# A 31-tap depthwise convolution: 8 of 31 taps on TensorE as diagonal matmuls, against 17 of 31 in four token phases

## The chip, the cores and the metric

The kernel runs on one core of one Trainium2 chip. The metric is the device time of the whole program in microseconds (us), as the median of several runs; a profile of one further execution gives the trace. The core's engines each run their own instruction stream in order: TensorE (PE, with its weight loads shown as PEld), VectorE (DVE), ScalarE (ACT), GpSimd (POOL) and SyncE (SP), from whose queue the DMA transfers of this kernel are issued. An engine waits for another by semaphores.

## The reference

Two layers of a network run over 1024 latent tokens and 128 context tokens with 1024 features. Only the mixer of the second (odd) layer matters here. It projects 1024 features to 1536: 512 conv inputs `a`, 512 gates, 512 pool inputs.

```python
def depthwise_conv(x, w, b):
    K = w.shape[0]                      # 31 taps
    y = lax.conv_general_dilated(x, w[:, None, :], window_strides=(1,),
                                 padding=[(K // 2, K // 2)],
                                 dimension_numbers=("NWC", "WIO", "NWC"),
                                 feature_group_count=x.shape[-1])
    return y + b

def odd_mixer(h, w_in, w_dw, b_dw, g_cn, w_pool, s_pool, w_out):
    z = h @ w_in
    a, gte, p = jnp.split(z, [CONV_W, 2 * CONV_W], axis=-1)   # 512, 512, 512
    conv = a * jax.nn.sigmoid(gte)
    conv = depthwise_conv(conv, w_dw, b_dw)
    conv = jax.nn.silu(rms_norm(conv, g_cn))
    pool = multi_scale_pool(p).reshape(B, L, POOL_GROUPS, POOL_CH)
    pool = jnp.einsum("blgc,gcd->blgd", pool, w_pool).reshape(B, L, POOL_W) * s_pool
    return jnp.concatenate([conv, pool], axis=-1) @ w_out
```

The rest of the program is the first layer's mixer (attention and a gated unit), a feed-forward part with a 3-tap convolution in each layer, and norms. Both kernels run it from the same code.

## The kernel before, in words

All activations lie with features on the 128 partitions and tokens along the free axis, in three blocks of 384, 384 and 386 tokens (`BLK`). Matmuls work on pairs of rounded fp32 tiles: each operand is split into a high part (ScalarE copies it to the format `F32R`) and a low part (VectorE subtracts), and `mm3` (L76 to L78) multiplies high by high, high by low and low by high into one PSUM tile. `split` (L83, L84) does this for activations, `unit` and `unit_split` (L58, L66, L67) for weights: a load by SP into a staging tile `raw` of the pool `wraw`, and a split into `wt`. Diagonals built by GpSimd used a tile of the same staging pool.

`odd` is the mixer. It runs twelve projections in the order conv 0, conv 1, pool 0, pool 1, conv 2, pool 2, pool 3, conv 3; a conv has two (gates and values), a pool group one. `proj` makes one: for each token block, 24 matmuls into an `ips` tile of PSUM and an evacuation: `sg` (sigmoid, L1079), `cv` (value times gate, L1093, VectorE), or `xp` (L1116). `cv` holds 128 channels with padding, 1198 wide. The output of a conv, `co`, is 1168 wide.

A conv of 128 channels is shared between two engines. The last 8 taps are matmuls: `conv_prep` lets GpSimd build 8 diagonal 128x128 matrices `dg` (L1157), splits them to `dp` and splits `cv` to `cs`; `conv_pe` multiplies 8 diagonals with 8 shifted views of `cs`, for three stretches of columns (390, 390, 388), into `cps` tiles which ScalarE evacuates into `co` with the bias (L1174). The other 23 taps are `conv_steps`: each is one VectorE instruction `co = cv * w + co` over 1168 columns (L1181). They come after `conv_pe` in the program, for they add to its result.

The order of the work is that of the program, as a scheduler with priorities lays it on each engine. Two lists spread work over it: `fill` holds the taps, and `drip(n)` emits n of them behind each projection block; `pend` holds the call that starts a conv's matmuls (`conv_go`), which is taken from the list in block `GOB` (1) of the next projection.

Then come two halves of the output projection: `out_half` with the pool groups' half first (`pool_out` splits the pooled sums to `ph`, multiplies with a 128x128 matrix into `pp`, and evacuates to `h`, L1224 and L1225), then the conv half, whose input `conv_tail` makes from `co` with a norm over the channels. In the first `out_half` the call `mid` issues conv 3's matmuls between the pool products and the output tiles `ops`.

## Time and profile before

| | |
|---|---|
| time, median of 3 runs | 2802.07 us (2801.71 to 2804.49) |
| profiled execution, its own time | 2798.91 us |
| span of its instructions | 2797.1 us |
| mean granted TensorE clock | 0.985 |
| the odd mixer in it | from 1589 us (first `ips` matmul) to some 1970 us |
| conv matmuls `cps` | 288, from 1635.1 to 1818.3 us |
| conv taps on VectorE | 92, 133.2 us busy |

Times in the trace are counted from the span's start. A row of a stretch gives each engine's busy time in it with the count of instructions in brackets, then the clock that TensorE was granted (1.00 is full), the busy share of the DMA engines and the bytes moved. A row of a tile gives the instructions that touch it: line, engine, operation, count, then minimum, median and maximum duration in ns, and the first and last start. A row of the timeline is start, duration, engine, line, operation, and in square brackets the idle time before it and what ended that. Matmuls overlap in the pipe, so their pace is the distance of successive starts, not the duration.

### The profile page before, as it was taken

Reading aid. Unit: us, or ns where it says so; the run is one execution under the profiler, and the core shown is the slowest. Engines: PE = TensorE matmul, PEld = TensorE weight load, DVE = VectorE, ACT = ScalarE, POOL = GpSimd, SP = SyncE. Lnnn points to the kernel's source line nnn. Section 1 sums busy time; section 2 is a strip of 40 time slices with the busy share of each in tenths; the row PEclk is TensorE's granted clock in tenths of the full one; section 3 lists DMA queues with packets and bytes.
Section 4 is the critical chain, followed back from the end, with each engine's and each line's share of the span. In section 5 each row is a group of like instructions: output and inputs, shape, how many; then the busy total and the mean of one; then the engine's idle time right before and its main releaser. Section 6 shows DMA issues by size and latency. Waiting matters only on the chain.

```text
span 2797.1 us, 38522 instructions
## 1 busy us (share of the span) xinstructions
PE 2702.6 (97%) x15444; PEld 2622.6 (94%) x15444; DVE 1889.4 (68%) x3120; ACT 1010.8 (36%) x1798; POOL 375.6 (13%) x433
## 2 busy tenths in 40 slices
PE   7999989999999999999999999989999999999999
PEld 3897978889999999999999999888999999999999
DVE  5873799998787788855453878887555455554445
ACT  3543278882343222222223331225422222222331
POOL 2354155540200010000000200002000000000000
PEclk9999999999999999999999999999999999999999
DMA  7254210007143444311111011011011111111111
GB/s 277 71 154 112 86 32 23 25 1 234 53 128 114 131 133 128 119 48 46 38 46 38 10 46 39 27 39 38 31 38 46 38 46 39 45 37 40 46 46 68
DMA packets 92851, 192.64 MB, mean 69 GB/s; under 512 B 9472, under 2 KB 43136, under 8 KB 92672
## 3 DMA queue, kind: packets, MB, share of 16 engines
q1 hardware_dynamic: 92672, 190.18, 21.3%
q8 instruction: 122, 2.00, 0.3%
q14 instruction: 57, 0.47, 0.1%
HBM read 170.20 MB, written 19.95 MB: 68 GB/s over the span
## 4 chain that ended last, share of the span: by engine, by line
PE 83%; DVE 10%; DMA 3%; ACT 2%; issue 1%; POOL 1%; SPq 0%; DVEq 0%; POOLq 0%; ACTq 0%
PE fps L76 13%; PE fps L77 13%; PE fps L78 13%; PE ops L76 8%; PE ops L78 8%; PE ops L77 8%; PE av L982 2%; DMA mraw<-in_wmod_dram 2%; PE ptp L971 1%; DVE macc L157 1%; PE ips L76 1%; PE ips L77 1%; PE ips L78 1%; PE Sa L995 1%; PE mps L126 1%
## 5 line engine op out<-in xcount | busy, mean ns | idle before, releaser
L76 PE MATMUL fps<-h,wt 128*128 128x384 f32 (+1 forms) x2112 | 711.8, 339 | 1.6 <-ACT z L401 1.2
L77 PE MATMUL fps<-h,wt 128*128 128x384 f32 (+1 forms) x2112 | 713.0, 338 | 0.0
L78 PE MATMUL fps<-h,wt 128*128 128x384 f32 (+1 forms) x2112 | 712.7, 338 | 0.0
L379 DVE SCALAR_TENSOR_TENSOR x<-ops,mod,x 128x384 f32<-128x384 f32 (+1 forms) x832 | 395.6, 513 | 235.3 <-PE ops L78 233.8
L67 DVE TENSOR_TENSOR wt<-raw,wt 128x1024 fp32r<-128x1024 f32 (+2 forms) x177 | 216.8, 1235 | 385.1 <-ACT wt L66 384.6
L77 PEld LDWEIGHTS fps<-h,wt 128*128 128x128 f32 x2112 | 398.6, 189 | 0.3
L76 PEld LDWEIGHTS fps<-h,wt 128*128 128x128 f32 x2112 | 396.2, 188 | 2.5 <-ACT z L401 1.5
L78 PEld LDWEIGHTS fps<-h,wt 128*128 128x128 f32 x2112 | 398.1, 189 | 0.0
L78 PE MATMUL ops<-act,wt 128*128 128x384 f32 (+1 forms) x1056 | 358.2, 339 | 0.0
L77 PE MATMUL ops<-act,wt 128*128 128x384 f32 (+1 forms) x1056 | 357.0, 338 | 0.0
L76 PE MATMUL ops<-act,wt 128*128 128x384 f32 (+1 forms) x1056 | 355.4, 339 | 0.0
L401 ACT ACTIVATE z<-fps 128x384 f32<-128x384 f32 (+1 forms) x264 | 129.0, 493 | 602.9 <-PE fps L78 602.6
L66 ACT ACTIVATE wt<-raw 128x1024 fp32r<-128x1024 f32 (+2 forms) x177 | 182.8, 1047 | 440.1 <-PE ops L78 316.2
L157 DVE SCALAR_TENSOR_TENSOR macc<-mraw,sc,macc 128x512 f32<-128x512 f32 x280 | 214.5, 796 | 42.1 <-DMA mraw<-in_wmod_dram 41.7
L76 PEld LDWEIGHTS ops<-act,wt 128*128 128x128 f32 x1056 | 199.6, 189 | 0.0
L77 PEld LDWEIGHTS ops<-act,wt 128*128 128x128 f32 x1056 | 198.7, 188 | 0.0
L78 PEld LDWEIGHTS ops<-act,wt 128*128 128x128 f32 x1056 | 198.6, 188 | 0.1
L1181 DVE SCALAR_TENSOR_TENSOR co<-cv,c_odw,co 128x1168 f32<-128x1168 f32 x92 | 133.2, 1451 | 19.1 <-ACT co L1174 18.2
L76 PE MATMUL ops<-h,wt 128*128 128x384 f32 (+1 forms) x384 | 132.7, 351 | 7.0 <-ACT h L83 5.4
L83 ACT ACTIVATE act<-c 128x1154 fp32r<-128x1154 f32 x44 | 51.5, 1171 | 227.9 <-DVE c L422 183.5
L77 PE MATMUL ops<-h,wt 128*128 128x384 f32 (+1 forms) x384 | 132.2, 344 | 0.9 <-DVE h L84 0.9
L410 DVE SCALAR_TENSOR_TENSOR c<-z,fdw,c 128x1153 f32<-128x1153 f32 x88 | 125.7, 1429 | 8.6 <-ACT c L408 7.7
(275 smaller groups left out, 4578.0 us busy)
## 6 DMA issues: line engine op xcount, KB each, us to landing
raw<-in_fin_dram SPq DMA_DIRECT2D x88, 512.0 KB, 3.6
mraw<-in_wmod_dram SPq DMA_DIRECT2D x160, 256.0 KB, 2.8
raw<-in_fout_dram SPq DMA_DIRECT2D x44, 512.0 KB, 3.5
mraw<-in_wmod_dram SPq DMA_DIRECT2D x16, 512.0 KB, 8.8
fold<-macc SPq DMA_DIRECT2D x14, 512.0 KB, 2.9
macc<-fold SPq DMA_DIRECT2D x56, 128.0 KB, 3.3
x<-in_xt_dram SPq DMA_DIRECT2D x4, 1536.0 KB, 10.3
raw<-in_odin_dram SPq DMA_DIRECT2D x12, 512.0 KB, 3.5
```

Source lines behind the costliest of these rows:

```text
L66: nc.scalar.activation(wt[:, 0, :n], raw[:, :n], AF.Copy)
L67: nc.vector.tensor_tensor(out=wt[:, 1, :n], in0=raw[:, :n], in1=wt[:, 0, :n].bitcast(F32), op=ALU.subtract)
L76: mm(out, wh, ah, start=start, stop=False)
L77: mm(out, wh, al, start=False, stop=False)
L78: mm(out, wl, ah, start=False, stop=stop)
L83: ins = nc.scalar.activation(hi, src, AF.Copy)
L157: nc.vector.scalar_tensor_tensor(out=a[:, c, :], in0=raw, scalar=self.sc[:, k, c:c + 1], in1=a[:, c, :], op0=ALU.mult, op1=ALU.add)
L379: nc.vector.scalar_tensor_tensor(out=xs, in0=ps[:, o:o + w], scalar=self.mod[l][:, gch * 8 + m, c:c + 1], in1=xs, op0=ALU.mult, op1=ALU.add)
L401: nc.scalar.activation(z[:, c0:c0 + n], ps[:, :n], AF.Copy)
L410: nc.vector.scalar_tensor_tensor(out=c[:, 1:T], in0=z[:, 0:T - 1], scalar=w[:, l, ti, 0:1], in1=c[:, 1:T], op0=ALU.mult, op1=ALU.add)
L982: nc.tensor.matmul(av[:, :256].rearrange("p (j t) -> p j t", j=2), V[:, kt, h, :], rhs, start=(kt == 0 and part == 0), stop=(kt == 8 and p ...
L1181: nc.vector.scalar_tensor_tensor(out=o, in0=cv[:, j:j + COW], scalar=dw[:, j:j + 1], in1=o, op0=ALU.mult, op1=ALU.add)
```

## The change

17 of the 31 taps (14 to 30) go to TensorE. The operands are laid out anew: four token phases (token number modulo 4) of 32 channels each stand on the 128 partitions, for four groups of 32 channels in turn. One 128x128 matrix then mixes four input phases into four output phases and covers up to four taps; five of them (`NM`), on views shifted by one, cover 17 taps. The matrices of a group (128x640 fp32, 328 KB, `odiag`) are made on the host as constants and loaded, 16 times in all.

For each conv, `conv_prep` now lets GpSimd copy `cv` into four phases (`by4`), writes that to DRAM (`cvx`), reads it back in four transfers with phases on the partitions (`xr`), and splits that to `xs`. `conv_pe` gives four steps. Step g loads the matrices of group g into a staging tile, splits them to `dp`, makes 15 matmuls of 128x292 into one `cps` tile and copies it to `yo`. After the fourth, `yo` goes to DRAM (`cvy`), comes back in four transfers as `yb`, and `conv_merge` adds it to `co` on VectorE with a stride of four. The tiles `by4`, `xr`, `yo`, `yb` and the pool's `win` have one tag and one buffer (`by4`), and `dp` has one.

The 14 taps left no longer wait for the matmuls: the first writes `co` with the bias (a `tensor_scalar`), and the merge adds the matmuls' part. `pend` gives one step per projection block, after `SKIP` = 2 empty ones; conv 3's steps stand in the first output half, one behind each output tile after `SKIP3` = 4 empty ones. `pool_windows` works in place, every second `ph` uses the tag `dp`, and the tiles `hb` are as wide as their block.

```diff
-                            if b == GOB and pend:
-                                pend.pop()()
+                            if pend:
+                                pend.pop(0)()
...
-                        while len(self.fill) > 31 - NPE:
+                        while len(self.fill) > 8:
...
                     def conv(i):
                         cv = conv_in(i)
-                        ops = self.conv_prep(cv, dw[:, i, :], pdt)
-                        pend.append(lambda: conv_go(i, cv, ops))
+                        self.fill += self.conv_steps(co[:, i, :], cv, dw[:, i, :])
+                        xs = self.conv_prep(i, cv, pdt)
+                        pend.extend([lambda: None] * SKIP + conv_go(i, xs))
...
+    def conv_prep(self, i, cv, pool):
+        by4 = pool.tile([P, 4, XN], F32, tag="by4", bufs=1, name=self.nm("by4"))
+        nc.gpsimd.tensor_copy(by4, cv[:, J0:J0 + 4 * XN].rearrange("p (n s) -> p s n", s=4))
+        d = self.dram.tile([P, 4, XN], F32, name=f"cvx{i}")
+        nc.sync.dma_start(out=d, in_=by4)
+        xr = pool.tile([P, 4, XN], F32, tag="by4", bufs=1, name=self.nm("xr"))
+        for q in range(4):
+            nc.sync.dma_start(out=xr[32 * q:32 * q + 32, :, :], in_=d[:, q, :].rearrange("(g c) n -> c g n", c=32))
+        xs = pool.tile([P, 2, 4, XN], F32R, tag="cs", bufs=1, name=self.nm("xs"))
+        self.split(xs[:, 0], xs[:, 1], xr)
+        return xs
+
+    def conv_pe(self, i, xs, pool, done):
...
+        def step(g):
+            if not yo:
+                yo.append(pool.tile([P, 4, YN], F32, tag="by4", bufs=1, name=self.nm("yo")))
+            raw = self.wraw.tile([P, 1024], F32, tag="raw", name=self.nm("raw"))
+            nc.sync.dma_start(out=raw[:, :NM * P], in_=self.ap["odiag"][4 * i + g])
+            wt = pool.tile([P, 2, NM * P], F32R, tag="dp", bufs=1, name=self.nm("dp"))
+            self.unit_split(wt, raw, NM * P, None)
+            ps = self.gp.tile([P, 512], F32, tag="gp", name=self.nm("cps"))
+            for m in range(NM):
+                self.mm3(ps[:, :YN], wt[:, 0, m * P:(m + 1) * P], wt[:, 1, m * P:(m + 1) * P],
+                         xs[:, 0, g, m:m + YN], xs[:, 1, g, m:m + YN], m == 0, m == NM - 1)
+            nc.scalar.activation(yo[0][:, g, :], ps[:, :YN], AF.Copy)
+            if g == 3:
+                d = self.dram.tile([P, 4, YN], F32, name=f"cvy{i}")
+                nc.sync.dma_start(out=d, in_=yo[0])
+                yb = pool.tile([P, 4, YN], F32, tag="by4", bufs=1, name=self.nm("yb"))
+                for h in range(4):
+                    nc.sync.dma_start(out=yb[32 * h:32 * h + 32, :, :], in_=d[:, h, :].rearrange("(q c) n -> c q n", c=32))
+                done(yb)
...
+    def conv_merge(self, o, yb):
+        o4 = o.rearrange("p (n q) -> p q n", q=4)
+        self.nc.vector.tensor_tensor(out=o4, in0=o4, in1=yb, op=ALU.add)
...
-            ph = tp.tile([P, 2, BW], F32R, tag="ph", name=self.nm("ph"))
+            ph = tp[g % 2].tile([P, 2, BW], F32R, tag=("ph", "dp")[g % 2], bufs=1, name=self.nm("ph"))
...
-NPE = 8
+NM = 5
+NPE = 4 * NM - 3
+J0 = 31 - NPE
+YN = COW // 4
+XN = YN + NM - 1
```

Three places show how the instructions stand on the engines. The numbers behind a tile's name tell tiles apart; they differ between the kernels.

The first is TensorE where a conv's matmuls begin or go from phase to phase. Before, at conv 1's start in the middle of the first pool projection (`ips_15650`, `ips_15756`: its token blocks 1 and 2), the three `cps` tiles of 24 matmuls each share one `dp`:

```order
L78 MATMUL ips_15650<-h_1132_6920,wt_15520 128x384
L76 MATMUL cps_15676<-cs_15613,dp_15610 128x390
L76 MATMUL cps_15702<-cs_15613,dp_15610 128x390
L76 MATMUL cps_15728<-cs_15613,dp_15610 128x388
L76 MATMUL ips_15756<-h_1133_6921,wt_15520 128x386
L77 MATMUL ips_15756<-h_1133_6921,wt_15520 128x386
```

After, from phase 0 to phase 1 of conv 0 (`cps_15446` with `dp_15443`, then `cps_15505` with `dp_15502`, and the next projection `ips_15524`):

```order
L77 MATMUL cps_15446<-xs_15349,dp_15443 128x292
L78 MATMUL cps_15446<-xs_15349,dp_15443 128x292
L76 MATMUL cps_15505<-xs_15349,dp_15502 128x292
L77 MATMUL cps_15505<-xs_15349,dp_15502 128x292
L76 MATMUL ips_15524<-h_1132_6920,wt_15355 128x384
```

The first two matmuls of a phase moved up to directly behind the last of the phase before, which used the same buffer of `dp`; 24 projection matmuls follow, and then the phase's other 13.

On ScalarE at the same place, before (the split of `dp_15610` for conv 1 stands behind the evacuations of conv 0's three tiles):

```order
L1079 ACTIVATE sg_15348<-ips_15380 128x384
L66 ACTIVATE wt_15619<-raw_15617 128x1024
L1174 ACTIVATE co<-cps_15406,c_odw 128x390
L1174 ACTIVATE co<-cps_15432,c_odw 128x390
L1174 ACTIVATE co<-cps_15458,c_odw 128x388
L83 ACTIVATE dp_15610<-dg_15608 128x1024
```

and after, the whole of conv 0 and the beginning of conv 1 (`yo_15440` is conv 0's output, `dp_15736` the first matrices of conv 1):

```order
L83 ACTIVATE xs_15349<-xr_15344 128x1184
L1185 ACTIVATE yo_15440<-cps_15446 128x292
L66 ACTIVATE dp_15502<-raw_15500 128x640
L1185 ACTIVATE yo_15440<-cps_15505 128x292
L66 ACTIVATE dp_15552<-raw_15550 128x640
L66 ACTIVATE wt_15647<-raw_15645 128x1024
L1185 ACTIVATE yo_15440<-cps_15555 128x292
L66 ACTIVATE dp_15603<-raw_15601 128x640
L66 ACTIVATE wt_15772<-raw_15770 128x1024
L1116 ACTIVATE xp_15644<-ips_15650 128x384
L1185 ACTIVATE yo_15440<-cps_15606 128x292
L66 ACTIVATE dp_15736<-raw_15734 128x640
```

Each split of the next phase's matrices now stands behind the evacuation of the phase before it.

The second place is the turn from conv 0 to conv 1. Before, SP's queue holds only loads of weights (`raw<-in_odin_dram`) there. After:

```order
L1188 DMA cvy_15623<-yo_15440 128x1168
L1178 DMA raw_15801<-in_odiag_dram 128x640
L1178 DMA raw_15851<-in_odiag_dram 128x640
L1191 DMA yb_15625<-cvy_15623 32x4x292 x4
L1160 DMA cvx_15634<-by_2183_15632 128x1184
L1163 DMA xr_15636<-cvx_15634 32x4x296 x4
```

and on TensorE, after, conv 1's first matmul (`cps_15739`, which reads `xs_15641`, the split of `xr_15636`):

```order
L77 MATMUL ips_15706<-h_1133_6921,wt_15471 128x386
L78 MATMUL ips_15706<-h_1133_6921,wt_15471 128x386
L76 MATMUL cps_15739<-xs_15641,dp_15736 128x292
L76 MATMUL ips_15775<-h_1131_6919,wt_15647 128x384
L77 MATMUL ips_15775<-h_1131_6919,wt_15647 128x384
```

Conv 0's way out through DRAM and conv 1's way in stand one after the other in the queue, with two loads of matrices between. On TensorE 46 projection matmuls (22 of `ips_15678`, 24 of `ips_15706`) lie between conv 0's last matmul and conv 1's first.

The third is VectorE behind the last projection, where conv 2's or conv 3's taps (L1181 before, L1202 and L1204 after) share it with the pool's `ph` and `h`. Before:

```order
L1093 TENSOR_TENSOR cv_16480<-ips_16558,sg_16390 128x128
L1181 SCALAR_TENSOR_TENSOR co<-cv_15993,c_odw,co 128x1168
L84 TENSOR_TENSOR ph_16611<-pd,ph_16611 128x384
L84 TENSOR_TENSOR ph_16620<-pd,ph_16620 128x384
L1181 SCALAR_TENSOR_TENSOR co<-cv_15993,c_odw,co 128x1168
L84 TENSOR_TENSOR cs_16591<-cv_16480,cs_16591 128x1198
L1225 SCALAR_TENSOR_TENSOR h_1131_6919<-pp_16614,c_odw,h_1131_6919 128x384
```

After:

```order
L1093 TENSOR_TENSOR cv_16539<-ips_16615,sg_16452 128x128
L67 TENSOR_TENSOR wt_16560<-raw_16558,wt_16560 128x512
L1202 TENSOR_SCALAR co<-cv_16539,c_odw 128x1168
L84 TENSOR_TENSOR ph_16671<-pd,ph_16671 128x384
L1204 SCALAR_TENSOR_TENSOR co<-cv_16539,c_odw,co 128x1168
L1249 SCALAR_TENSOR_TENSOR h_1131_6919<-pp_16683,c_odw,h_1131_6919 128x384
L84 TENSOR_TENSOR ph_16698<-pd,ph_16698 128x384
L1249 SCALAR_TENSOR_TENSOR h_1131_6919<-pp_16674,c_odw,h_1131_6919 128x384
L1204 SCALAR_TENSOR_TENSOR co<-cv_16539,c_odw,co 128x1168
```

Conv 3's own taps moved up to this place, one for every one or two steps of the pool's chain, 11 of them ahead of the first output tile; conv 2's are done by then.

More of the change, by code (lines that the diff above doesn't have):

```diff
@@ L554, in out_half @@
         make(0)
-        if mid:
-            mid()
         if not late:
@@ L577, in out_half @@
                         self.out_tile(x, l, 2, b, m, terms)
+                        if mid:
+                            mid.pop(0)()
                         self.drip(drip)
@@ L1130, in odd @@
                     cv = conv_in(3, last)
-                    ops = self.conv_prep(cv, dw[:, 3, :], pdt)
+                    self.fill += self.conv_steps(co[:, 3, :], cv, dw[:, 3, :])
+                    xs3 = self.conv_prep(3, cv, pdt)
                 wps = units.pop()
@@ L1136, in odd @@
                     self.out_half(x, l, ap["odout"][1], hb, 4,
-                                  lambda b: self.at(PRP, self.pool_out, b, pd, dw, hb[b][:, :, 4:8, :], tp, wps), drip=DRIP2, ws=units,
-                                  mid=lambda: conv_go(3, cv, ops), outer=True)
+                                  lambda b: self.at(PRP, self.pool_out, b, pd, dw, hb[b][:, :, 4:8, :], (tp, pdt), wps), drip=DRIP2, ws=units,
+                                  mid=[lambda: None] * SKIP3 + conv_go(3, xs3), outer=True)
                 pdp.close()
@@ L1150, in odd @@
                                       late=True, extra=extra)
-    def conv_prep(self, cv, dw, pool):
+    def conv_prep(self, i, cv, pool):
         nc = self.nc
-        dg = self.wraw.tile([P, NPE, P], F32, tag="raw", name=self.nm("dg"))
-        nc.gpsimd.tensor_tensor(out=dg, in0=self.ident.unsqueeze(1).to_broadcast([P, NPE, P]),
-                                in1=dw[:, 31 - NPE:31].unsqueeze(2).to_broadcast([P, NPE, P]), op=ALU.mult)
-        dp = pool.tile([P, 2, NPE, P], F32R, tag="dp", bufs=1, name=self.nm("dp"))
-        self.split(dp[:, 0], dp[:, 1], dg)
-        cs = pool.tile([P, 2, CVW], F32R, tag="cs", bufs=1, name=self.nm("cs"))
-        self.split(cs[:, 0, :], cs[:, 1, :], cv)
-        return dp, cs
@@ L1165, in conv_pe @@
-    def conv_pe(self, o, ops, dw):
-        dp, cs = ops
-        for c1, c2 in ((0, 390), (390, 780), (780, COW)):
-            ps = self.gp.tile([P, 512], F32, tag="gp", name=self.nm("cps"))
-            for a in range(NPE):
-                j = 31 - NPE + a
-                self.mm3(ps[:, :c2 - c1], dp[:, 0, a, :], dp[:, 1, a, :], cs[:, 0, c1 + j:c2 + j], cs[:, 1, c1 + j:c2 + j],
-                         a == 0, a == NPE - 1)
-            self.nc.scalar.activation(o[:, c1:c2], ps[:, :c2 - c1], AF.Identity, bias=dw[:, 31:32])
+        by4 = pool.tile([P, 4, XN], F32, tag="by4", bufs=1, name=self.nm("by4"))
@@ new lines, in conv_prep @@
+        self.split(xs[:, 0], xs[:, 1], xr)
+        return xs
+    def conv_pe(self, i, xs, pool, done):
+        nc = self.nc
+        yo = []
+        def step(g):
[5 more added lines that the diff above has]
+            self.unit_split(wt, raw, NM * P, None)
+            ps = self.gp.tile([P, 512], F32, tag="gp", name=self.nm("cps"))
+            for m in range(NM):
[9 more added lines that the diff above has]
+                done(yb)
+        return [lambda g=g: step(g) for g in range(4)]
@@ L1180, in tap @@
         def tap(j):
-            nc.vector.scalar_tensor_tensor(out=o, in0=cv[:, j:j + COW], scalar=dw[:, j:j + 1], in1=o, op0=ALU.mult, op1=ALU.add)
+            if j == 0:
+                nc.vector.tensor_scalar(out=o, in0=cv[:, 0:COW], scalar1=dw[:, 0:1], scalar2=dw[:, 31:32], op0=ALU.mult, op1=ALU.add)
+            else:
+                nc.vector.scalar_tensor_tensor(out=o, in0=cv[:, j:j + COW], scalar=dw[:, j:j + 1], in1=o, op0=ALU.mult, op1=ALU.add)
         return [lambda j=j: tap(j) for j in range(31 - NPE)]
+    def conv_merge(self, o, yb):
+        o4 = o.rearrange("p (n q) -> p q n", q=4)
+        self.nc.vector.tensor_tensor(out=o4, in0=o4, in1=yb, op=ALU.add)
     def pool_windows(self, g, xp, icnt, pd, w1):
@@ L1194, in pool_windows @@
         cur, s, L = xp, 1, W
-        pp = w1.tile([P, 2, CVW], F32, tag="cs", bufs=1, name=self.nm("win"))
-        i = 0
+        nx = w1.tile([P, 4 * XN], F32, tag="by4", bufs=1, name=self.nm("win"))
         while s < w:
             L -= s
-            nx = pp[:, i % 2, :]
-            i += 1
             nc.vector.tensor_tensor(out=nx[:, :L], in0=cur[:, :L], in1=cur[:, s:s + L], op=ALU.add)
@@ L1274, in new_hb @@
     def new_hb(self):
-        return [self.hpool.tile([P, 2, KT, BW], F32R, tag=f"h{b}", name=self.nm(f"h{b}")) for b in range(3)]
+        return [self.hpool.tile([P, 2, KT, BLK[b][1]], F32R, tag=f"h{b}", name=self.nm(f"h{b}")) for b in range(3)]
     def run(self):
@@ L1330 @@
 CVCH = 512
-GOB = 1
+SKIP = 2
+SKIP3 = 4
 GDRIP = 6
@@ L1415, in layout @@
     out["odw"] = np.ascontiguousarray(od.reshape(34, 4, P).transpose(2, 1, 0))
+    w = a["od_w_dw"][0].reshape(31, 16, 32)
+    dg = np.zeros((16, 4, 32, NM, 4, 32), f)
+    ch = np.arange(32)
+    for si in range(4):
+        for m in range(NM):
+            for so in range(4):
+                j = 4 * m + si - so
+                if 0 <= j < NPE:
+                    dg[:, si, ch, m, so, ch] = w[J0 + j]
+    out["odiag"] = dg.reshape(16, P, NM * P)
     out["owp"] = np.ascontiguousarray(a["od_w_pool"][0].transpose(1, 0, 2)).reshape(P, 512)
```

5 lines of the change are left out of this document (2 added, 3 removed).

## The prediction

> **What bounds the kernel now.** I read the page's shares first, then the stretches of the convolution's layer, then its tiles one by one. The profiled execution took 2798.91 us, 3.2 below the runs' median of 2802.07; the sum below is made against it and 3.2 is added at the end.
>
> ```profile
> span 2797.1 us, 38522 instructions
> PE 2702.6 (97%) x15444; PEld 2622.6 (94%) x15444; DVE 1889.4 (68%) x3120; ACT 1010.8 (36%) x1798; POOL 375.6 (13%) x433
> ```
>
> TensorE is the bound of the whole. VectorE, from which the change takes taps, ends the time only where TensorE stands still. The stretches say where that is (columns: stretch, its length, busy time of each engine, granted clock, DMA share, GB/s):
>
> ```profile
> core 0: us, PE busy (x) PEld busy (x) DVE busy (x) ACT busy (x) POOL busy (x), PEclk, DMA share, GB/s
> 1625.00:1790.00 165.00, 163.45 (x925) 163.37 (x926) 135.72 (x135) 34.31 (x53) 11.42 (x21) 1.00 0.12 41
> 1790.00:1800.00 10.00, 4.91 (x19) 3.56 (x17) 10.00 (x17) 4.53 (x9) 0.11 (x1) 0.82 0.33 106
> 1880.00:1897.00 17.00, 9.24 (x38) 7.98 (x37) 10.75 (x22) 8.00 (x13) 1.71 (x2) 0.70 0.38 122
> ```
>
> From 1625 to 1790 (projections and convs 0 to 2) TensorE is idle for 1.55 of 165 us and VectorE has 29 us to spare: taps taken off VectorE there are worth nothing, and every wait put before a TensorE matmul costs its full length. Its 925 matmuls there give the pace of the projections, 163.45/925 = 0.177 us. Only after 1790 does VectorE (10.00 of 10.00 busy) hold TensorE up.
>
> **Fewer and smaller matmuls (a gain).** Before, each conv is 72 matmuls of 390 columns; after, 4 phases x 15 of 292. The pace is in successive starts, of this conv and of the nearest narrow product:
>
> ```profile
> 1811.04 0.34 PE L76 MATMUL cps<-cs,dp 128*128 128x390 f32 x1
> ...
> 1812.83 0.34 PE L77 MATMUL cps<-cs,dp 128*128 128x390 f32 x1
> 91.26 0.29 PE L652 MATMUL kvps<-wt,h 128*128 128x288 f32 x1
> ...
> 92.45 0.29 PE L652 MATMUL kvps<-wt,h 128*128 128x288 f32 x1
> ```
>
> ```profile
> L76 PEld LDWEIGHTS cps<-cs,dp x96: 187/188/334, 1635.0 to 1817.8; 128*128 128x128 f32 x96
> ```
>
> Ten steps in 1.79 us are 0.179; nine in 1.19 are 0.132 for 288 columns, so 0.1335 for 292. 288 x 0.1785 = 51.4 becomes 240 x 0.1335 = 32.0: **-19.4**. Were the weight load's 188 ns the pace, the matmuls would stay at some 0.1785, 42.8 in all, a gain of 8.6: a rival.
>
> **The taps.** 36 fewer on VectorE.
>
> ```profile
> L1181 DVE SCALAR_TENSOR_TENSOR co<-cv,c_odw,co 128x1168 f32<-128x1168 f32 x92 | 133.2, 1451 | 19.1 <-ACT co L1174 18.2
> L84 DVE TENSOR_TENSOR dp<-dg,dp x4: 1207/1218/1226, 1623.8 to 1788.7; 128x1024 fp32r<-128x1024 f32 x4
> L67 DVE TENSOR_TENSOR wt<-raw,wt 128x1024 fp32r<-128x1024 f32 (+2 forms) x177 | 216.8, 1235 | 385.1 <-ACT wt L66 384.6
> L66 ACT ACTIVATE wt<-raw 128x1024 fp32r<-128x1024 f32 (+2 forms) x177 | 182.8, 1047 | 440.1 <-PE ops L78 316.2
> L655 ACT ACTIVATE kv<-kvps x9: 396/413/430, 55.4 to 100.4; 128x288 f32<-128x288 f32 x9
> ```
>
> 36 x 1.45 = 52 less; 16 splits of 640-wide tiles (1.235 x 640/1024 = 0.78 each) add 12.5, in place of 4 x 1.22 = 4.9; four merges add 5.6: net some -39 us, hidden behind TensorE until 1790, so **0** there.
>
> **Waits between phases (a loss).** The split weights `dp` have one buffer. Phase g+1's split can only begin when phase g's last matmul is done, and ACT's order puts the evacuation `yo` ahead of it. From the rows above: 0.41 (288 wide) + 1.047 x 640/1024 = 0.68, and the tail of a matmul (0.29 long at a pace of 0.13), some 0.4 with the signal: 1.5 us. In TensorE's order the first two matmuls of g+1 stand right behind g's last, or behind two projection matmuls (0.35). The 24 projection matmuls that could hide the split stand behind these two. Twelve such places: conv 0 1.5, 1.5, 1.15; conv 1 three of 1.15; conv 2 1.5, 1.3, 1.15; conv 3 0 (behind three output tiles), 1.5, 1.5: **+14.6** (0.9 to 1.35 each on the mean: 11 to 16). The second operand, VectorE's half, has those 24 matmuls as its cover (4.2 us against 0.78 and one tap); behind two taps it wouldn't hold.
>
> **Conv 1's two trips through DRAM (a loss).** `by4`, `xr`, `yo` and `yb` share one buffer. Conv 1's rearrangement can't begin before conv 0's result has gone out, come back and been merged. The nearest row of a trip is the fold of 512 KB (ours are 592 and 584), and prices of the two strided copies lie between these:
>
> ```profile
> L163 SPq DMA_DIRECT2D fold<-macc x14: 326/327/327, 666.8 to 1187.0; - x14
> L167 POOL TENSOR_TENSOR macc<-macc x14: 1280/1607/2531, 674.7 to 1195.3; 128x512 f32<-128x512 f32 x14
> fold<-macc SPq DMA_DIRECT2D x14, 512.0 KB, 2.9
> macc<-fold SPq DMA_DIRECT2D x56, 128.0 KB, 3.3
> L955 POOL TENSOR_SCALAR P<-P,ast 128x384 f32<-128x384 f32 x192 | 109.5, 586 | 145.1 <-DVE ast L953 49.7 <-ACT P L946 25.6 <-DMA qkr<-kd 15.9
> L1157 POOL TENSOR_TENSOR dg<-ident,c_odw x4: 1900/2956/4361, 1606.7 to 1782.8; 128x1024 f32<-128x1024 f32 x4
> L1201 DVE TENSOR_TENSOR win<-xp 128x1183 f32<-128x1183 f32 x4 | 5.5, 1386 | 0.2 <-ACT xp L1116 0.2
> L83 ACT ACTIVATE cs<-cv x4: 1187/1192/1208, 1629.6 to 1797.3; 128x1198 fp32r<-128x1198 f32 x4
> ```
>
> The last fold leaves at 1187.0 and its sum starts at 1195.3: 8.3 for out and back (the first 7.9; 6.2 from the two landings alone). The copy to four phases on GpSimd: 586 x 1184/384 = 1.8 at least, 4.36 (the slowest diagonal) at most; 2.5, nearer the pure copy. The merge is the 1183-wide add, 1.4, at most twice that. Chain: 0.3 + 0.41 + 8.3 + 1.4 + 2.5 + 8.3 + 1.2 = 22.4 us from conv 0's last matmul to conv 1's first, and TensorE's order has 46 projection matmuls between: 46 x 0.177 = 8.1. It stands still for 14.3, after which the clock must come back. The trace has such a pause:
>
> ```profile
> 1791.83 0.34 PE L78 MATMUL ips<-h,wt 128*128 128x386 f32 x1
> 1797.03 1.10 PE L76 MATMUL pp<-ph,wt 128*128 128x384 f32 x2 [4.87 <-ACT ph L83]
> 1800.00:1805.00 5.00, 4.49 (x13) 4.09 (x14) 5.00 (x7) 1.15 (x3) 0.00 (x0) 0.50 0.00 0
> 1826.73 0.53 PE L76 MATMUL ops<-h,wt 128*128 128x384 f32 x1
> ```
>
> After 4.87 us of rest the clock is 0.50; I take 5 us at half, 2.5 lost: **+16.8** (11 with 6.2 a trip, 1.8 for the copy and 1.7 for the clock; 23 with 9.6 a trip by size and the upper copies).
>
> [...]
>
> **The other convs.** At conv 0's start ACT splits `dp` ahead of the gates, and VectorE evacuates `cv`:
>
> ```profile
> 1622.69 1.06 ACT L83 ACTIVATE dp<-dg 128x1024 fp32r<-128x1024 f32 x1 [0.60 <-DVE h L88]
> 1626.53 1.55 DVE L1093 TENSOR_TENSOR cv<-ips,sg 128x384 f32<-128x384 f32 x4 [0.39 <-ACT sg L1079]
> ```
>
> That split is gone there (1.06 and its wait of 0.60): TensorE starts 1.6 earlier. Its first phase then waits: 1.6 evacuation + 2.5 + 8.3 + 1.2 = 13.6, and some 1.7 (half a landing) on SP behind three weight loads, less 72 projection matmuls (12.7): 2.6. Together **+1** (-1.6, if the trip is hidden, to +5). Conv 2's trip (12.0) has three projection blocks (12.7) as its cover, but a window add in the shared buffer (1.39) and two evacuations hold a projection's PSUM buffer for some 2.3, and the trip's start may cost 0.2: **+2.5** (0 to 6).
>
> **The stretch after the projections.** Before: 1791.83 to 1826.73, 35 us with 19.2 of full-rate matmul work (72 conv matmuls, 36 of the pool), 15.9 lost. After: conv 3's matmuls stand in the output stage, some 6 remain. VectorE's pace there, in successive starts:
>
> ```profile
> 1824.01 0.62 DVE L1225 SCALAR_TENSOR_TENSOR h<-pp,c_odw,h 128x386 fp32r<-128x386 f32 x1
> 1824.54 0.55 DVE L84 TENSOR_TENSOR ph<-pd,ph 128x386 fp32r<-128x386 f32 x1
> 1825.01 1.43 DVE L1181 SCALAR_TENSOR_TENSOR co<-cv,c_odw,co 128x1168 f32<-128x1168 f32 x1
> 1826.35 0.62 DVE L1225 SCALAR_TENSOR_TENSOR h<-pp,c_odw,h 128x386 fp32r<-128x386 f32 x1
> ```
>
> ```profile
> DVE h L1225 <- ACT h L1224: 4.8, 2, 4.0
> ```
>
> 0.53 an `h`, 0.47 a `ph`, 1.34 a tap. After the change 11 taps, 12 `ph`, 8 `h`, the split of `xs` (1.4) and half a weight split (0.6) stand ahead of the first output tile: 14.7 + 5.6 + 4.2 + 2.0 = 26.5, so 20.5 lost: **+4.5** (-1 with four taps later in the queue, to +9 with the waits for `h` of before, 4.8, on top).
>
> **The end.** Between the halves TensorE loses time behind `rb` and `h`:
>
> ```profile
> 1886.48 1.65 PE L286 MATMUL rb<-dg,ones 128*128 128x384 f32 x2 [4.75 <-DVE dg L284]
> 1892.21 2.29 PE L76 MATMUL ops<-h,wt 128*128 128x384 f32 x6 [3.01 <-ACT h L83]
> ```
>
> With the clock, the stretch 1880 to 1897 loses 17 - 9.24 x 0.70 = 10.5. Conv 3's sum is ready 1.4 after `yb`, without a tap behind it, three taps (4.0) sooner than now: 6.5 lost. A weight split on ACT behind a norm is late by its own 1.05 and a signal, 1.5: **-2.5** (-7 to +3).
>
> **Sum:** -19.4 + 14.6 + 16.8 + 1 + 2.5 + 4.5 - 2.5 = +17.5; 2798.9 + 17.5 = 2816.4, as a median 2819.6; I say 2819.5.
>
> **Rivals.**
> *Not slower: the lighter VectorE pays after 1790.* If output tiles and pool products no longer queue behind taps, the stretch shrinks to what `ph` and `h` alone need (12 x 1.0 us with 6 of work, 6 lost: -9.9 in place of +4.5) and the end's 10.5 vanish (in place of -2.5): 17.5 - 14.4 - 8 = -4.9, a median of 2797. For: VectorE 10.00 of 10.00 busy there. Against: the order still has eleven taps between those steps. It decides once the two together give 12 us more than I count.
> *Slower still: SP's queue.* Loads of diagonals wait for staging buffers ahead of `xr` and `yb` in SP's order; if each conv's trip stands 4 us (a landing, 3.3, and an issue) behind one: +16, 2835. For: one queue issues all of it. Against: their splits mostly precede the transfers.
> *The narrow matmuls buy less.* The weight load sets the pace: 10.8 less gain, 2830. For: 188 ns a load; against: 0.132 in the row above.
>
> **How the numbers follow.** A measurement of this kernel can tell about 0.2%, 5.6 us, from no change. Forecast 0.60 (own range 2808 to 2829); VectorE's relief 0.18; SP 0.14; narrow matmuls 0.08. The forecast's terms move by some 9 together. All but 2 in 10 lies from 2799 to 2835. Faster by over 0.2% needs the relief and short trips: 0.09 in all; within 0.2%: the rest of the relief and the forecast's low edge, 0.13; slower 0.78.
>
> **What would show it.** Twelve rests of 1.2 to 1.5 us before `cps` released by ACT `dp`; one of 11 to 20 before conv 1's first, with the clock at half behind it; `cps` starts 0.133 apart; the first output tile about 26 after the last projection. I am wrong if the trips take half of 8.3, if conv 1's rest is under 8, or if the pool stretch falls below 20.

## The result and the profile after

The changed kernel takes 2825.72 us (median of 4 runs, 2820.88 to 2827.8) against 2801.89 before in the same runs: ratio 1.0081, 95% interval 1.0063 to 1.0098, 23.8 us slower. The forecast was 17.5 slower, 2819.5. The profiled execution has a span of 2825.6 us, 28.5 more than the one before. From the page of the changed kernel:

```profile
span 2825.6 us, 38562 instructions
PE 2686.5 (95%) x15396; PEld 2602.0 (92%) x15396; DVE 1859.5 (66%) x3100; ACT 1015.7 (36%) x1814; POOL 373.7 (13%) x433
```

TensorE is busy for 16.1 us less and VectorE for 29.9 less, and yet the span grew: TensorE rests more, and what it does it does in part at a slower clock (mean 0.975 against 0.985). The stretches of the odd mixer (from the first projection matmul; TensorE restarts with the third projection, conv 1's gates, at 1623.5; last projection matmul at 1822.7; first output tile at 1852.7; first feed-forward matmul at 1985.3; the borders are whole microseconds beside these):

```profile
core 0: us, PE busy (x) PEld busy (x) DVE busy (x) ACT busy (x) POOL busy (x), PEclk, DMA share, GB/s
1589.00:1623.00 34.00, 30.41 (x152) 27.31 (x152) 31.75 (x68) 19.61 (x38) 5.89 (x12) 0.95 0.00 1
1623.00:1823.00 200.00, 162.69 (x900) 158.40 (x900) 125.06 (x124) 38.51 (x65) 9.18 (x22) 0.91 0.29 89
1823.00:1853.00 30.00, 14.83 (x35) 9.22 (x35) 29.36 (x45) 13.37 (x26) 2.63 (x1) 0.54 0.17 52
1853.00:1904.00 51.00, 48.75 (x285) 48.27 (x285) 23.55 (x37) 9.44 (x19) 3.70 (x4) 0.97 0.18 54
```

Before, 1625 to 1790 had TensorE idle for 1.55 us at a clock of 1.00. Now, in the second row, 37 of 200 us are idle and the clock is 0.91. In the third VectorE is busy for 29.36 of 30 us, and TensorE works at a clock of 0.54. By the starts named above, and the same points before:

| stretch, us | before | after | difference | forecast |
|---|---|---|---|---|
| first projection matmul to restart | 37.4 | 35.7 | -1.8 | -1.6 |
| restart to last projection matmul | 165.3 | 199.2 | +33.9 | +18.9 |
| to the first output tile | 34.9 | 30.0 | -4.9 | -8.5 |
| to the first feed-forward matmul | 126.1 | 132.6 | +6.5 | +8.5 |

The sum is +33.7. The span grew by 28.5 only, for 5.2 came back in code whose text did not change (1.2 ahead of the mixer, 4.0 behind it); the part on the prediction says by what.

The main rests of the second stretch, from TensorE's timeline (conv 0's first matmul, one phase, conv 1's first, two projections held by the evacuation `xp`, one more phase):

```profile
1642.44 0.61 PE L76 MATMUL cps<-xs,dp 128*128 128x292 f32 x1 [4.46 <-ACT xs L83]
1652.61 0.40 PE L76 MATMUL cps<-xs,dp 128*128 128x292 f32 x1 [1.18 <-ACT dp L66]
...
1698.18 0.61 PE L76 MATMUL cps<-xs,dp 128*128 128x292 f32 x1 [15.85 <-ACT xs L83]
...
1739.68 0.44 PE L76 MATMUL ips<-h,wt 128*128 128x384 f32 x1 [2.84 <-ACT xp L1116]
1774.03 0.40 PE L76 MATMUL cps<-xs,dp 128*128 128x292 f32 x1 [1.18 <-ACT dp L66]
1808.80 0.69 PE L76 MATMUL ips<-h,wt 128*128 128x384 f32 x1 [5.24 <-ACT xp L1116]
```

Conv 1's wait, from conv 0's last evacuation on, all engines but TensorE:

```profile
1674.31 0.41 ACT L1185 ACTIVATE yo<-cps 128x292 f32<-128x292 f32 x1 [0.24 <-PE cps L78]
...
1674.75 0.33 SPq L1188 DMA_DIRECT2D cvy<-yo  x1
...
1677.91 2.78 SPq L1191 DMA_DIRECT2D yb<-cvy  x4
...
1683.76 2.22 DVE L1210 TENSOR_TENSOR co<-co,yb 128x1168 f32<-128x1168 f32 x1 [2.44 <-DMA yb<-cvy]
...
1686.10 3.35 POOL L1158 COPY by<-cv 128x1184 f32<-128x1184 f32 x1 [18.41 <-DVE co L1210]
1689.47 0.34 SPq L1160 DMA_DIRECT2D cvx<-by  x1
...
1696.94 1.19 ACT L83 ACTIVATE xs<-xr 128x1184 fp32r<-128x1184 f32 x1 [14.02 <-DMA xr<-cvx]
```

And the clock around these rests and at the restart (columns as above):

```profile
1623.54:1628.54 5.00, 5.00 (x19) 4.88 (x20) 4.84 (x5) 2.39 (x4) 2.34 (x1) 0.66 0.22 69
1640.00:1645.00 5.00, 2.56 (x8) 2.56 (x9) 2.84 (x3) 1.19 (x1) 0.00 (x0) 0.62 0.01 2
1645.00:1650.00 5.00, 5.00 (x23) 5.00 (x23) 2.01 (x3) 0.00 (x0) 0.00 (x0) 0.70 0.00 0
1695.00:1700.00 5.00, 1.82 (x6) 1.82 (x7) 2.92 (x3) 1.19 (x1) 0.20 (x3) 0.50 0.17 38
1700.00:1705.00 5.00, 5.00 (x25) 5.00 (x24) 0.00 (x0) 0.00 (x0) 0.00 (x0) 0.74 0.01 2
1740.00:1745.00 5.00, 5.00 (x22) 5.00 (x21) 2.56 (x2) 1.40 (x4) 0.00 (x0) 0.66 0.69 181
1810.00:1815.00 5.00, 5.00 (x26) 5.00 (x25) 1.46 (x1) 0.00 (x0) 0.00 (x0) 0.81 0.68 170
```

In the chain each step starts with the end of the one before: 9.0 us for the trip out, 2.2 for the merge, 3.4 for the copy, 7.5 for the trip in, 1.2 for the split. GpSimd's row says what it waited for: VectorE's merge, 18.41 us.

### The profile page after: what moved, and what is told of

The parts are those of the page before. It is cut to its first block, busy times and chain, and to the rows that moved or that the text cites. A ratio compares the mean times of both kernels' runs of the same rounds, so it can differ in the third digit from the quotient of the medians.

```text
span 2825.6 us, 38562 instructions
## 1 busy us (share of the span) xinstructions
PE 2686.5 (95%) x15396; PEld 2602.0 (92%) x15396; DVE 1859.5 (66%) x3100; ACT 1015.7 (36%) x1814; POOL 373.7 (13%) x433
## 4 chain that ended last, share of the span: by engine, by line
PE 80%; DVE 10%; DMA 5%; ACT 2%; issue 1%; POOL 1%; SPq 0%; DVEq 0%; ACTq 0%; POOLq 0%
PE fps L76 13%; PE fps L77 13%; PE fps L78 13%; PE ops L76 8%; PE ops L77 8%; PE ops L78 8%; PE av L982 2%; DMA mraw<-in_wmod_dram 2%; DVE macc L157 1%; PE ptp L971 1%; PE Sa L995 1%; PE ips L76 1%; PE mps L126 1%; PE ips L77 1%; PE ips L78 1%
## 5 line engine op out<-in xcount | busy, mean ns | idle before, releaser
L76 PE MATMUL ops<-h,wt 128*128 128x384 f32 (+1 forms) x384 | 132.4, 353 | 8.5 <-ACT h L83 7.6
L77 PE MATMUL ops<-h,wt 128*128 128x384 f32 (+1 forms) x384 | 132.8, 346 | 0.2 <-DVE h L84 0.2
L78 PE MATMUL ops<-h,wt 128*128 128x384 f32 (+1 forms) x384 | 130.9, 343 | 0.0
## 6 DMA issues: line engine op xcount, KB each, us to landing
x<-in_xt_dram SPq DMA_DIRECT2D x4, 1536.0 KB, 10.1
```

The lines of the kernel that those rows point to most:

```text
L76: mm(out, wh, ah, start=start, stop=False)
L77: mm(out, wh, al, start=False, stop=False)
L78: mm(out, wl, ah, start=False, stop=stop)
```

## The experiments

In the table, "lost" is the time between two successive matmul starts less what the first takes at full pace (0.1765 us a projection matmul, as before the change, 0.1335 a conv matmul), between restart and last projection, for every gap over 0.5 us. The total is that whole stretch less 720 and 180 matmuls at these paces; what it has beyond the named gaps is mainly slow clock. In the changed kernel the gaps make 38.8 of 48.0, and the clock in the rows above some 9: 2.5 behind conv 0's rest, 2.2 behind conv 1's, 2.7 behind the two at `xp`, and 1.7 behind a rest of 2.60 at the restart. "Behind" is the stretch from last projection to first output tile.

| | ratio to before (interval) | conv 0's first | phases of conv 0 to 2 | conv 1's first | behind `xp` | total lost | behind |
|---|---|---|---|---|---|---|---|
| before | 1 | 0 | 0 | 0 | 0 | 0 | 34.9 |
| after | 1.0081 (1.0063 to 1.0098) | 4.6 | 9.8 | 16.0 | 8.4 | 48.0 | 30.0 |
| e1 | 1.0079 (1.0064 to 1.0094) | 0 | 10.1 | 16.4 | 8.6 | 46.5 | 29.2 |
| e2 | 0.9988 (0.9978 to 0.9997) | 4.6 | 11.1 | 4.2 | 0 | 25.1 | 26.6 |
| e3 | 1.0030 (1.0018 to 1.0043) | 3.3 | 10.2 | 16.5 | 0 | 34.3 | 28.0 |
| e4 | 0.9982 (0.9972 to 0.9991) | 4.3 | 0 | 11.8 | 0.6 | 23.6 | 31.4 |
| e5 | 1.0060 (1.0044 to 1.0077) | 4.5 | 9.8 | 16.4 | 8.8 | 49.6 | 23.1 |
| e6 | 0.9987 (0.9978 to 0.9997) | 0 | 6.3 | 7.4 | 0 | 18.0 | 32.6 |
| e7 | 1.0053 (1.0038 to 1.0068) | 0 | 8.8 | 16.3 | 8.9 | 41.5 | 27.2 |
| e10 | 0.9913 (0.9899 to 0.9928) | 0 | 6.7 | 0 | 0 | 10.1 | 22.7 |

**e1: a control that frees a buffer's room.**

```diff
-                pd = pdt.tile([P, 4, T], F32, name="pd")
+                pd = pdt.tile([P, 3, T], F32, name="pd")
...
-            out = pd[:, g, o:o + n]
+            out = pd[:, min(g, 2), o:o + n]
```

> Control for the next three. The changed kernel, but pool group 3 is written over pool group 2 (their sums share one place in pd, which leaves group 2 out of the output): that frees 4.6 KB per partition and moves no instruction. All theories: the time of the changed kernel, 2825.7 us, ratio to before 1.0085 within 0.002.

Measured: ratio 1.0079 (1.0064 to 1.0094), as the changed kernel. The next three contain this edit and are read against it. In its profile conv 0's rest is missing from the table because TensorE rested longer just ahead, 1.79 and 2.79 us for late weight splits at the restart; the total is close to the changed kernel's all the same.

**e2: a buffer for `yo` and `yb`.**

```diff
-                yo.append(pool.tile([P, 4, YN], F32, tag="by4", bufs=1, name=self.nm("yo")))
+                yo.append(pool.tile([P, 4, YN], F32, tag="yo", bufs=1, name=self.nm("yo")))
...
-                yb = pool.tile([P, 4, YN], F32, tag="by4", bufs=1, name=self.nm("yb"))
+                yb = pool.tile([P, 4, YN], F32, tag="yo", bufs=1, name=self.nm("yb"))
```

> As e1, and yo and yb have a buffer of their own instead of sharing by4's. Theory (one shared buffer makes conv 1's way in wait for conv 0's way out, and the pool windows wait for a conv's way out): conv 1's rest of 15.85 us and its slow clock (2.2) go, and the two rests behind xp (2.84 and 5.24, with 2.8 of slow clock) go: 18 + 11 = 29 us less than e1, some 2797, ratio 0.998. Rival 1 (SP's queue holds the transfers behind loads of matrices): the rest before conv 1 stays above 8 us and the time above 2810. Rival 2 (VectorE is late with the second half of the split): rest between 3 and 8 us, 2803 to 2810.

Ratio 0.9988 (0.9978 to 0.9997): 0.0091 less than the control, 25 us of the 29. Both rests behind `xp` are gone, and conv 1's fell from 16.4 to 4.2. The copy now ran at 1662.1, long before conv 0's last evacuation. What is left points to rival 1's cause, though at 4.2 not with its size (over 8). From SP's timeline of this run:

```profile
1666.35 0.36 SPq L1160 DMA_DIRECT2D cvx<-by  x1
1672.17 0.33 SPq L1188 DMA_DIRECT2D cvy<-yo  x1
1672.91 3.26 SPq L1163 DMA_DIRECT2D xr<-cvx  x4
```

The read `xr` of a `cvx` issued at 1666.35 stood behind `cvy`, which waited for conv 0's `yo` until 1672.17. That in turn was late on ScalarE: conv 0's last matmul began at 1668.63, but its evacuation stood behind a weight split that had waited for its load:

```profile
1670.40 1.06 ACT L66 ACTIVATE wt<-raw 128x1024 fp32r<-128x1024 f32 x1 [8.33 <-DMA raw<-in_odin_dram]
1671.74 0.41 ACT L1185 ACTIVATE yo<-cps 128x292 f32<-128x292 f32 x1
```

So the shared buffer made three quarters of conv 1's rest. That the order of the queues makes the remaining quarter is read from these rows; no run changes it alone.

**e3: a buffer for the pool's window sums.**

```diff
-        nx = w1.tile([P, 4 * XN], F32, tag="by4", bufs=1, name=self.nm("win"))
+        nx = w1.tile([P, 4 * XN], F32, tag="win", bufs=1, name=self.nm("win"))
```

> As e1, and the pool's window sums have a buffer of their own instead of sharing by4's. Theory: conv 1's rest of 15.85 stays; the two rests behind xp (2.84 and 5.24 with their slow clock, 11 in all) go: some 2815, ratio 1.0047. Rival (those rests come from VectorE's own backlog, not from the shared buffer): no change, 2825.

1.0030: 0.0049, 14 us less than the control. The rests behind `xp` are gone, and conv 1's is what it was:

```profile
1689.87 0.61 PE L76 MATMUL cps<-xs,dp 128*128 128x292 f32 x1 [16.32 <-ACT xs L83]
```

The chain behind `xp` is therefore the shared buffer's too: a window sum waits until the conv's `yo` has left its place, the pool's `xp` (one buffer) waits for the sum before, and projection tiles stay in PSUM until TensorE has none left.

**e4: two buffers for `dp`.**

```diff
-            wt = pool.tile([P, 2, NM * P], F32R, tag="dp", bufs=1, name=self.nm("dp"))
+            wt = pool.tile([P, 2, NM * P], F32R, tag="dp", bufs=2, name=self.nm("dp"))
...
-            ph = tp[g % 2].tile([P, 2, BW], F32R, tag=("ph", "dp")[g % 2], bufs=1, name=self.nm("ph"))
+            ph = tp[g % 2].tile([P, 2, BW], F32R, tag=("ph", "dp")[g % 2], bufs=(1,2)[g%2], name=self.nm("ph"))
```

> As e1, but the split matrices dp have two buffers. Theory (the split of the next phase's matrices waits for the last matmul of this phase): the eleven rests of 0.78 to 1.18 us between phases go, 9.8 us and 0.16 each, so 11 less: some 2814, ratio 1.0045; conv 1's rest stays or grows by what conv 0 gains. Rival (the matrices arrive late: the staging buffers, not dp, hold them): the rests stay, 2825.

0.9982: 0.0097, 27 us less than the control, more than twice the expected 11. All rests between phases are gone, as the theory has it. But the others shrank too:

```profile
1684.41 0.61 PE L76 MATMUL cps<-xs,dp 128*128 128x292 f32 x1 [11.60 <-ACT xs L83]
```

Conv 1's four phases last 23.4 us, from first to last matmul, where they took 30.7 in the control. Only 3.1 of these 7.3 are the rests. The second buffer also changed TensorE's order: the first two matmuls of a phase no longer move up to the phase before, and 72 projection matmuls stand inside conv 1 in place of 94. So conv 1's output leaves the shared buffer earlier, and the rests behind `xp` fall from 8.6 to 0.6. The chain from conv 0's last to conv 1's first matmul is as long as before (24.5 against 24.6 us), but 72 projection matmuls in place of 46 lie beside it, worth 4.6, which is what conv 1's rest lost. So 27 us is the price of the single buffer with the order that comes of it; the eleven rests alone are 12.7 of it (10.1 in convs 0 to 2, 2.6 in conv 3), and no run parts the two.

**e5: conv 3's taps behind the pool's chain.**

```diff
+                if getattr(self, "last_h", None):
+                    self.follow(ins, self.last_h, "the pool goes first")
```

(`ins` is a conv's first tap, `last_h` the pool's latest write of `h`.)

> The changed kernel, but conv 3's fourteen taps may start only behind the last step of the pool's chain (one added dependency). Theory (behind the last projection VectorE's taps stand between the pool's steps, one for each, 4.68 us a pair, and hold TensorE, which rests so much that its clock stays at half): the stretch from the last projection to the first output tile falls from 30 to some 16 us, the taps (19 us) fit beside the 51 us of output tiles, so 13 less than the changed kernel: ratio 1.0035. Rival (the taps are only paid later: conv 3's sum is late for the norm): the stretch falls but the end grows by as much, ratio 1.008.

1.0060 (1.0044 to 1.0077): some 6 us less than the changed kernel, half of what was expected; the two intervals overlap, so the stretch is the better witness. It fell from 30.0 to 23.1, not to 16, and the end did not grow (first output tile to feed-forward 130.8, after 132.6). The taps did hold TensorE. What holds it without them, on this run's timeline of TensorE and then of ScalarE:

```profile
1828.88 1.01 PE L76 MATMUL pp<-ph,wt 128*128 128x384 f32 x2 [1.32 <-ACT ph L83]
1832.50 1.01 PE L76 MATMUL pp<-ph,wt 128*128 128x384 f32 x2 [1.32 <-ACT ph L83]
```

```profile
1826.96 0.58 ACT L1250 ACTIVATE h<-pp,c_odw 128x384 fp32r<-128x384 f32 x1 [1.74 <-PE pp L78]
1827.44 0.51 ACT L83 ACTIVATE ph<-pd 128x384 fp32r<-128x384 f32 x1
```

A pair of products takes 3.62 us in place of 4.68, with TensorE at a clock of 0.50 (from 1825 to 1840). On ScalarE (second fence) the next `ph` stands behind an `h` that waits 1.74 for TensorE's product, and TensorE then waits for that `ph`: a round through two engines that the expectation left out.

**e6: SKIP = 5.**

```diff
-SKIP = 2
+SKIP = 5
```

> The changed kernel with SKIP = 5 in place of 2: three more projection blocks stand between a conv's rearrangement and its first matmul; 116 projection matmuls (20.5 us) instead of 46 (8.1) between conv 0's last and conv 1's first. Theory (the chain of 24.5 us from conv 0's last matmul to conv 1's first is fixed, and only too short a cover makes it a rest): conv 1's rest falls from 16 to 4, conv 0's 4.6 goes, with their slow clock some 19 less, 2806 or ratio 1.001. Rival (the later steps make the pool windows, which share the buffer, later too, and TensorE rests there instead): the rests behind xp grow from 8 to over 15, ratio above 1.005.

0.9987 (0.9978 to 0.9997): 26 us less than the changed kernel from one number. Conv 0's rest is gone. Before conv 1 the operand is ready at 1687.6, yet TensorE rests there, for another reason:

```profile
1699.73 0.61 PE L76 MATMUL cps<-xs,dp 128*128 128x292 f32 x1 [7.20 <-ACT xp L1116]
```

Here the rival is right on the spot though not on the sum: the window sum, which shares the buffer, started only at 1695.85, and the next `xp` could begin only behind it.

**e7: the four-phase copy on ScalarE.**

```diff
-        nc.gpsimd.tensor_copy(by4, cv[:, J0:J0 + 4 * XN].rearrange("p (n s) -> p s n", s=4))
+        nc.scalar.activation(by4, cv[:, J0:J0 + 4 * XN].rearrange("p (n s) -> p s n", s=4), AF.Copy)
```

> The changed kernel, but ScalarE makes the four-phase copy by4 instead of GpSimd. In the changed kernel's trace a VectorE instruction that runs beside GpSimd's copy takes 2.2 us longer than its like (weight split 3.40 against 1.22, first tap 3.13 and 2.87 against 0.88). Theory (the copy on GpSimd costs its own 2.3 to 3.4 us on the chain and holds VectorE): the copy takes 1.2 to 2.4 on ScalarE, the long VectorE rows are gone, conv 1's rest falls by 1 to 2, the pool stretch by 2: 3 to 5 less, ratio 1.0065. Rival (ScalarE's queue waits at the copy for conv 0's merge, and what stands behind it is late): no gain or a loss, 1.008 to 1.010.

1.0053 (1.0038 to 1.0068): 8 us less than the changed kernel, more than the 3 to 5 expected. Conv 1's rest did not change (16.3). What went is conv 0's 4.6 and its slow clock: in the changed kernel `cvx` left at 1630.62, 3.1 after the copy's end, behind a load of matrices issued at 1630.19, when the split that freed a staging buffer had ended (a late one: VectorE's split ahead of it ran 3.40 us beside the copy); here it stood ahead of such a load and left with the copy's end, at 1620.55. The first tap, beside which GpSimd no longer copies, is short in all four convs (first row the changed kernel, second row this one):

```profile
L1202 DVE TENSOR_SCALAR co<-cv,c_odw x4: 877/1878/3128, 1628.6 to 1826.4; 128x1168 f32<-128x1168 f32 x4
```

```profile
L1202 DVE TENSOR_SCALAR co<-cv,c_odw x4: 882/886/912, 1619.3 to 1811.7; 128x1168 f32<-128x1168 f32 x4
```

**e8: four edits together.** They are those of e5 and e7, `yo` and `yb` of convs 0 to 2 in `pd`'s last group, and this:

```diff
-            wt = pool.tile([P, 2, NM * P], F32R, tag="dp", bufs=1, name=self.nm("dp"))
+            wt = pool.tile([P, 2, NM * P], F32R, tag=("dp", "by4")[g % 2 if i < 3 else 0], bufs=1, name=self.nm("dp"))
```

> The whole computation, with four edits together: yo and yb of convs 0 to 2 in the place that pool group 3 fills only later (in pd), the split matrices of convs 0 to 2 in turn in dp's and by4's buffer, the copy on ScalarE, conv 3's taps behind the pool's chain. Theory, in the sums of the single edits: 25 (own yo) + 10 (phase rests of convs 0 to 2) + 13 (taps) less than the changed kernel: some 2774, ratio 0.990 to before. Rival (the rests share the same cover, so that the gains overlap): above 0.995.

0.9951 (0.9936 to 0.9966): just on the rival's side of its 0.995, with an interval that spans it. Conv 2's merge here reads what pool group 3 has already written in that place, so part of the output is another. Matrices in `by4`'s buffer now waited for the pool's window sums: one gap of 10.0 us between conv 2's phases, where the changed kernel had 1.3.

**e9: the kernel before with 14 taps.**

```diff
-        return [lambda j=j: tap(j) for j in range(31 - NPE)]
+        return [lambda j=j: tap(j) for j in range(14)]
```

> The kernel before with only 14 of the 23 VectorE taps of each conv: taps 14 to 22 are left out of the result. It prices VectorE's relief alone, with the old matmuls. Theory (until the last projection the taps lie beside TensorE's work and are worth nothing; only behind it do they hold the pool's chain and the norm): the stretch up to the last projection stays within 2 us, the stretch behind it and the end give 5 to 12: ratio 0.996 to 0.998. Rival (the taps hold TensorE all along, so that the changed kernel's lighter VectorE is worth 20 us and more and its layout costs that much more than thought): ratio below 0.993.

0.9963 (0.9949 to 0.9977), as the theory has it. Restart to last projection stayed at 165.3 us though VectorE had some 25 us less to do there. The row below has the same times as the prediction's row of before (135.72 busy). But this run restarts 4.2 later, at 1630.7; from 1629.2 to 1794.2 its VectorE is busy for 110.50:

```profile
1625.00:1790.00 165.00, 162.05 (x917) 161.29 (x916) 109.24 (x117) 36.46 (x57) 10.48 (x28) 1.00 0.12 41
```

The stretch behind fell by 5.9, the one up to the first feed-forward matmul by 2.6. Nine taps of each conv are worth 8.5 us by the trace, some 10 by the ratio, and in the trace all of it lies behind the last projection.

**e10: a version that beats both.** The edits of e5 and e7, phase 1 of conv 0 in `by4`'s buffer, and:

```diff
-                pd = pdt.tile([P, 4, T], F32, name="pd")
+                pdl = pdt.tile([P, 4 * T + COW - T], F32, name="pd")
+                pd = pdl[:, :4 * T].rearrange("p (g t) -> p g t", g=4)
+                self.ytmp = pdl[:, 3 * T:3 * T + COW].rearrange("p (g n) -> p g n", g=4)
...
+                        if g == 3:
+                            while pend:
+                                pend.pop(0)()
+                            self.drip(len(self.fill))
```

(Behind the last pool projection come the merges first, then group 3's windows.)

> The whole computation of the changed kernel, with yo and yb of convs 0 to 2 in the place that pool group 3 fills only afterwards, the copy on ScalarE, conv 3's taps behind the pool's chain, and phase 1 of conv 0 split into by4's idle buffer. Theory (sums of the single edits, each less the overlap): own yo 25, copy 7, taps 5, two phase rests 2.5: 39 less than the changed kernel, ratio 0.994. Rival (overlap: the edits remove the same rests): 0.997 or more.

2777.76 us (2775.09 to 2779.76), 0.9913 of before (0.9899 to 0.9928): 22 us less than the kernel before, and 47 less than the changed one, where the single edits let expect 39. Conv 0's and conv 1's first matmuls wait only 0.27 and 0.12 for their operands; five gaps of 0.8 to 2.1 between phases are left, 10.1 lost in all. The gain over the kernel before is not all the convolution's: some 14 us of the 22 come, by an estimate in the next part, from narrower `hb` tiles, which this kernel has too. From its page:

```profile
span 2775.2 us, 38546 instructions
PE 2673.2 (96%) x15396; PEld 2591.6 (93%) x15396; DVE 1848.3 (67%) x3100; ACT 1024.7 (37%) x1818; POOL 364.3 (13%) x430
```

**e11: the same with SKIP = 3.**

```diff
-SKIP = 2
+SKIP = 3
```

> As e10, without the idle buffer for phase 1, and with SKIP = 3: one more projection block (4.2 us) between each rearrangement and its first matmul. Theory (with the shared buffer out of the way, what is left of conv 1's rest, some 4 us, is too short a cover): 3 to 5 less than e10 after its 2.5 are given back, ratio 0.993. Rival (the later steps hold other buffers longer and TensorE rests elsewhere): 0.995 or more.

0.9917 (0.9901 to 0.9932), not to be told from e10. Conv 0's merge here comes behind conv 1's output in the same place and reads that. There was no rest left before conv 1 for the longer cover to take, so the expected gain had nothing to come from.

## Why the prediction was right, and which terms were off

The side held, and so did most of the mechanisms; the total of 23.8 against 17.5, inside the own range of 2808 to 2829, came out in part by luck. In the profiles the mixer's four stretches grew by 33.7, where the terms give 17.3. What brought the total back is a part of the change that the forecast put at nothing: the tiles `hb` are as wide as their block, and these tiles feed matmuls in the whole program, not in the mixer alone. Before, all three were 386 wide; now two are 384.

```profile
L76 PE MATMUL fps<-h,wt x2112: 332/339/633, 740.1 to 2740.5; 128*128 128x384 f32 x131, 128*128 128x386 f32 x61
L76 PE MATMUL fps<-h,wt x2112: 332/336/632, 742.9 to 2769.1; 128*128 128x384 f32 x131, 128*128 128x386 f32 x61
```

(First row before, second after: matmuls of the two feed-forward parts.) By successive starts, the 5904 matmuls of 384 columns that read `h` are 175.8 ns apart in the two profiles with the old tiles (before and e9) and 173.3 in all eleven with the new. The 386-wide ones, whose tile kept its width, are 177.0 and 177.2 apart, and 384-wide ones that read another tile (`act`) 175.6 in all. So an estimate is 5904 x 2.5 ns less and 2952 x 0.2 more, 14 us less in the program. That agrees with the parts outside the mixer: ahead of it 1580.7 to 1587.9 us with the new tiles against 1589.1 and 1593.3, behind it 839.3 to 840.5 against 844.3 and 844.6. No run changes this width alone, and why it matters to TensorE stays open. The terms:

- *Matmuls, -19.4.* Right, and the rival of the narrow matmuls fell. Twelve steps in 1.60 us are 0.1333, against 0.1335 forecast:

```profile
1711.66 0.29 PE L78 MATMUL cps<-xs,dp 128*128 128x292 f32 x1
...
1713.26 0.30 PE L78 MATMUL cps<-xs,dp 128*128 128x292 f32 x1
```

- *Waits between phases, +14.6.* Eleven rests of 0.78 to 1.18: 9.8 lost in convs 0 to 2 and 2.6 in conv 3, 12.4. e4 shows the cause: with a second buffer they are gone. What it gains beyond them comes with another order of the matmuls.
- *Conv 1's two trips, +16.8.* 16.0 lost and, from clocks of 0.50 and 0.74 in the 10 us around the restart, some 2.2 more: 18.2. The chain was 24.2, not 22.4: trips of 9.0 and 7.5 for twice 8.3, the merge 2.2 for 1.4, the copy 3.4 for 2.5. The 1.7 for the clock at the low edge of this term is shown by no run; the measured loss of some 2.2 stands in its place. e2 shows the cause.
- *Conv 0, +1.* Half a landing behind SP's loads was too little: `cvx` left 3.1 late, and 4.6 was lost where 2.6 was forecast, with some 2.5 of slow clock that the term did not have. That is the rival of SP's queue, true in this one place (e7, which also frees VectorE of the copy) and, by the rows, in e2's rest, not as 4 us on each conv.
- *Conv 2, +2.5.* The term that failed by most. It saw one projection held behind a window sum for 2.3. There were two rests, 3.0 and 5.4 lost, and each let the clock fall (0.66 from 1740 to 1745, 0.81 from 1810 to 1815): some 11 in the changed kernel, and 14 in e3, which takes them away. The step behind it was wrong too: it counted a window add and two evacuations, but what came late was the buffer, held by a conv's `yo` until that had left for DRAM. At the first of the two rests the sum waits for that transfer, and the next `xp` for the sum:

```profile
1735.87 1.39 DVE L1225 TENSOR_TENSOR win<-xp 128x1183 f32<-128x1183 f32 x1 [4.11 <-DMA cvy<-yo]
1739.14 1.32 ACT L1116 ACTIVATE xp<-ips 128x384 f32<-128x384 f32 x4 [8.25 <-DVE pd L1235]
```

- *The restart.* No term. A rest of 2.60 there let the clock fall (0.66 in the 5 us behind it, 1.7 lost); before the change one of 2.70 had not (1.00).
- *The stretch behind the last projection, +4.5.* 30.0 us in place of 26.5. The pace was as forecast, 4.68 a pair; the start was not: the last `cv` took 1.5 to evacuate, and the first tap ran 2.87 us beside GpSimd's copy instead of 0.88. e5 and e9 show that taps hold TensorE there.
- *The end, -2.5.* With conv 3's matmuls and waits 8.5 were forecast for the last stretch; it grew by 6.5. The rest of 4.75 behind `rb` is gone and the next one grew from 3.01 to 5.23; counted with the clock, 1875 to 1900 lost 11.2 before and 1900 to 1930 loses 8.5 now, so the norm's gain of 2.5 came out at 2.7.
- *The rival of the lighter VectorE* fell because the change put taps into the same place; e9 prices the relief with the old matmuls at some 10 us, and moving the taps away (e5) gains some 6.
